# The last input tile's weights: one early load, or fifteen loads of a few partitions behind the fourth store

## The chip, the core and the metric

The kernel runs on one core of a Trainium2 chip. The core has compute engines with instruction queues of their own (the vector engine, DVE; the scalar engine, ACT; the tensor engine, PE; GpSimd, POOL), the SyncE queue (SP), and 16 DMA engines that move data between the chip's main memory (HBM) and the on-chip memory of 128 partitions. DMA transfers are issued by instructions on SyncE's and ScalarE's queues. The metric is the time of one execution on the device in microseconds (us); less is better. Before the change the median of three runs is 240.65 us (240.62 to 240.68).

## What is computed

Every token's row of 512 float32 numbers is written out twice, each copy multiplied by one of the token's two weights. The expert indices are an input but are not used.

```python
batch, seq, hidden, n_experts = 16, 1024, 512, 8     # k = 2
x_expanded = x[:, :, np.newaxis, :].repeat(k, axis=2)
weights = expert_weights[..., np.newaxis]
return (x_expanded * weights).astype(np.float32)
```

That is 33.55 MB of x in, 0.13 MB of weights in, and 67.11 MB out. There is one multiplication for each number written.

## The kernel before

The 16,384 tokens are spread over 128 partitions, 128 tokens to a partition. The work is cut into six input tiles: five of 24 tokens for each partition and a last one of 8 (`groups`, line 32). An input tile (`x_tile`, two buffers) is filled by DMAs that ScalarE's queue issues (line 82): the first tile in six pieces of 4 tokens, every other tile in one transfer. `load(i + 2)` at line 119 asks for the tile after next, once tile `i` has been worked through.

For each token and each of its two weights, one instruction multiplies a 128x512 block by one column of `w_tile` and writes it into an output buffer (`o_tile`, two buffers, 12 tokens each). Column `c` of `w_tile` is the counter: where `c % 3 == 2` ScalarE does it (line 100), otherwise VectorE (line 106), so that VectorE has 16 and ScalarE 8 of the 24 blocks in an output buffer. When a buffer is full, SyncE issues one store of it (line 115): two stores for each tile of 24 tokens and one for the last tile, eleven in all, ten of 6,144 KB and one of 4,096 KB. Buffers are used in turn, so the buffer of store 4 is written again for store 6, that of store 5 for store 7.

The weights come in three loads at the start, all issued by SyncE ahead of the stores: those of the first tile (line 53, 48 columns), those of the next four tiles (line 54, 192 columns), and those of the last tile (line 58, 16 columns: 64 bytes for each of 128 partitions).

Instructions of one queue run in the order in which they stand. The order and all semaphore waits are made by the framework that builds the kernel from this text: an instruction waits for the data it reads and for the buffer it overwrites. In the trace's records every DMA issue names the semaphore on which it counts, and the waits of an instruction name the semaphores waited for. There are eight of them for DMA transfers, and one each for ScalarE's and VectorE's instructions.

The change is around lines 58 (removed), 115 (the store, whose instruction is kept in a name) and 119 (after it).

Of the kernel before, what the change touches and what calls it, by code (L numbers as in the profile page):

```python
# [1 line left out]

# [4 lines left out]


@with_exitstack
def kernel(  # L10
    ctx: ExitStack,
    tc: tile.TileContext,
    x: bass.AP,
    expert_indices: bass.AP,
    expert_weights: bass.AP,
    out: bass.AP,
):
    nc = tc.nc

    batch, seq, hidden = x.shape  # L20
    k = expert_weights.shape[-1]
    P = nc.NUM_PARTITIONS
    ntok = batch * seq
    assert ntok % P == 0
    A_TOTAL = ntok // P

    f32 = mybir.dt.float32
    row = k * hidden
    TX = 24
    TO = 12  # L30

    groups = [[24], [24], [24], [24], [24], [8]]
    assert sum(sum(g) for g in groups) == A_TOTAL

    xf = x.rearrange("b s h -> (b s) h")
    of = out.rearrange("b s k h -> (b s) (k h)")
    wf = expert_weights.rearrange("b s k -> (b s) k")

    w_pool = ctx.enter_context(tc.tile_pool(name="w_pool", bufs=1))
    x_pool = ctx.enter_context(tc.tile_pool(name="x_pool", bufs=2))  # L40
    o_pool = ctx.enter_context(tc.tile_pool(name="o_pool", bufs=2))

    w_tile = w_pool.tile([P, A_TOTAL * k], f32)

    def rows(of_all, done, T):
        return of_all[done * P : (done + T) * P, :].rearrange(
            "(p a) n -> p (a n)", a=T
        )

    T0 = sum(groups[0])  # L50
    G = len([g for g in groups[1:] if sum(g) == T0])
    head = (1 + G) * T0
    nc.sync.dma_start(out=w_tile[:, : T0 * k], in_=rows(wf, 0, T0))
    nc.sync.dma_start(
        out=w_tile[:, T0 * k : head * k].rearrange("p (g n) -> p g n", g=G),
        in_=wf[T0 * P : head * P, :].rearrange("(g p a) n -> p g (a n)", g=G, p=P),
    )
    nc.sync.dma_start(
        out=w_tile[:, head * k :], in_=rows(wf, head, A_TOTAL - head)
    )  # L60

    tiles = []
    done = 0
    for group in groups:
        T = sum(group)
        a0 = 0
        for n in group:
            tiles.append((done, T, a0, n))
            a0 += n
        done += T  # L70

    loaded = []

    def load(i):
        if i >= len(tiles):
            return
        done, T, a0, n = tiles[i]
        x_tile = x_pool.tile([P, TX * hidden], f32)
        src = rows(xf, done, T)
        step = TX // 6 if i == 0 else n  # L80
        for at in range(0, n, step):
            nc.scalar.dma_start(
                out=x_tile[:, at * hidden : (at + step) * hidden],
                in_=src[:, (a0 + at) * hidden : (a0 + at + step) * hidden],
            )
        loaded.append(x_tile)

    for i in range(2):
        load(i)
    for i, (done, T, a0, n) in enumerate(tiles):  # L90
        x_tile = loaded[i]
        outr = rows(of, done, T)
        for t in range(n):
            if t % TO == 0:
                o_tile = o_pool.tile([P, TO * row], f32)
            for kk in range(k):
                c = (done + a0 + t) * k + kk
                o = t % TO * row + kk * hidden
                if c % 3 == 2:
                    nc.scalar.mul(  # L100
                        out=o_tile[:, o : o + hidden],
                        in_=x_tile[:, t * hidden : (t + 1) * hidden],
                        mul=w_tile[:, c : c + 1],
                    )
                    continue
                nc.vector.tensor_scalar(  # L106
                    out=o_tile[:, o : o + hidden],
                    in0=x_tile[:, t * hidden : (t + 1) * hidden],
                    scalar1=w_tile[:, c : c + 1],
                    scalar2=None,  # L110
                    op0=mybir.AluOpType.mult,
                )
            if (t + 1) % TO == 0 or t + 1 == n:
                at = t // TO * TO
                nc.sync.dma_start(  # L115
                    out=outr[:, (a0 + at) * row : (a0 + t + 1) * row],
                    in_=o_tile[:, : (t + 1 - at) * row],
                )
        load(i + 2)

# [1 line left out]
_INS = ['x', 'expert_indices', 'expert_weights']  # L122
_OUTS = [((16, 1024, 2, 512), 'float32')]


# [23 lines left out]
```

## Time and profile before

| what | value |
|---|---|
| median of three runs | 240.65 us |
| span of the profiled execution (its own time; the profile lists no other) | 238.9 us |
| data moved | 100.81 MB, 422 GB/s over the span |
| DVE busy | 69.0 us, 171 instructions of 0.48 us |
| ACT busy | 54.9 us, 85 multiplications of 0.71 us and one table load |
| stores | 11, from issue to landing 33.6 us in the median of the ten large |
| x loads | 11, of which 6 pieces of the first tile |
| weights loads | 96, 24 and 8 KB; 11.1, 2.9 and 13.2 us from issue to landing |
| issue of the stores on SyncE | 13.38 us for the first, 218.4 us for the last |

The span begins with the first instruction of the program and ends with the last. A line of the chain of waits gives start, duration and what the time was spent on. A line of the timeline gives start, stretch, engine (a q marks the engine's queue, where DMA issues and semaphore instructions stand), line, operation and tiles, how many of them, and in square brackets the idle time ahead of the first one with what ended it. A line of the table of stretches gives the stretch, its length, the busy time of DVE, ACT and POOL with the number of instructions, the clock of the tensor engine (not used here), the mean busy share of the DMA engines, and GB/s. The DMA share of a short stretch can come out a little over 1. In the page, the DMA row gives the busy share in tenths in 40 slices of 5.97 us, where 9 is 90% or more.

### The profile page before, as it was taken

Reading aid. Unit: us, or ns where it says so; the run is one execution under the profiler, and the core shown is the slowest. Engines: PE = TensorE matmul, PEld = TensorE weight load, DVE = VectorE, ACT = ScalarE, POOL = GpSimd, SP = SyncE. Lnnn points to the kernel's source line nnn. Section 1 sums busy time; section 2 is a strip of 40 time slices with the busy share of each in tenths; the row PEclk is TensorE's granted clock in tenths of the full one; section 3 lists DMA queues with packets and bytes.
Section 4 is the critical chain, followed back from the end, with each engine's and each line's share of the span. In section 5 each row is a group of like instructions: output and inputs, shape, how many; then the busy total and the mean of one; then the engine's idle time right before and its main releaser. Section 6 shows DMA issues by size and latency. Waiting matters only on the chain.

```text
span 238.9 us, 364 instructions
## 1 busy us (share of the span) xinstructions
DVE 69.0 (29%) x171; ACT 54.9 (23%) x86; POOL 0.2 (0%) x4
## 2 busy tenths in 40 slices
DVE  0890300004609100190063037003706406415000
ACT  0870300004308000170071034003406106213000
POOL 0000000000000000000000000000000000000000
DMA  6999999999999999999999999999989899999994
GB/s 244 420 443 395 495 395 395 494 428 395 428 494 395 413 494 411 395 446 469 403 411 502 395 420 453 436 411 428 469 379 496 381 428 469 436 411 428 436 439 197
DMA packets 3986, 100.81 MB, mean 422 GB/s; under 512 B 1168, under 2 KB 1168, under 8 KB 1168
## 3 DMA queue, kind: packets, MB, share of 16 engines
q1 hardware_dynamic: 2400, 67.24, 65.2%
q10 hardware_dynamic: 1584, 33.56, 33.1%
q14 instruction: 2, 0.02, 0.0%
HBM read 33.69 MB, written 67.11 MB: 422 GB/s over the span
## 4 chain that ended last, share of the span: by engine, by line
DMA 66%; DVE 13%; another core or an unknown queue 11%; issue 0%; DVEq 0%; SPq 0%
DMA out_dram<-o_tile 54%; DVE o_tile L106 13%; DMA x_tile<-in_x_dram 11%; DVEq L144 0%; DVEq L106 0%; SPq L115 0%
## 5 line engine op out<-in xcount | busy, mean ns | idle before, releaser
L106 DVE TENSOR_SCALAR o_tile<-x_tile,w_tile 128x512 f32<-128x512 f32 x171 | 69.0, 480 | 149.3 <-DMA out_dram<-o_tile 105.3
L100 ACT ACTIVATE o_tile<-x_tile,w_tile 128x512 f32<-128x512 f32 x85 | 53.6, 709 | 155.5 <-DMA out_dram<-o_tile 116.8
L100 ACT ACT_TABLE_LOAD x1 | 1.3, 1283 | 6.7 <-DMA x_tile<-in_x_dram 6.7
L133 POOL MEMSET const-bfloat16-1.0<- 128x1 bf16 x1 | 0.1, 101 | 0.0
L133 POOL MEMSET const-uint8-127<- 128x1 uint8 x1 | 0.1, 101 | 0.0
L133 POOL MEMSET const-float32-0.0<- 128x1 f32 x1 | 0.1, 98 | 0.2 <-issue 0.2
L133 POOL MEMSET const-float32-1.0<- 128x1 f32 x1 | 0.1, 98 | 0.0
## 6 DMA issues: line engine op xcount, KB each, us to landing
out_dram<-o_tile SPq DMA_DIRECT2D x10, 6144.0 KB, 33.6
x_tile<-in_x_dram ACTq DMA_DIRECT2D x4, 6144.0 KB, 43.9
x_tile<-in_x_dram ACTq DMA_DIRECT2D x6, 1024.0 KB, 10.6
out_dram<-o_tile SPq DMA_DIRECT2D x1, 4096.0 KB, 19.5
x_tile<-in_x_dram ACTq DMA_DIRECT2D x1, 2048.0 KB, 24.0
w_tile<-in_expert_weights_dram SPq DMA_DIRECT2D x1, 96.0 KB, 11.1
w_tile<-in_expert_weights_dram SPq DMA_DIRECT2D x1, 24.0 KB, 2.9
w_tile<-in_expert_weights_dram SPq DMA_DIRECT2D x1, 8.0 KB, 13.2
```

What stands on the lines that cost most here:

```text
L100: nc.scalar.mul(out=o_tile[:, o : o + hidden], in_=x_tile[:, t * hidden : (t + 1) * hidden], mul=w_tile[:, c : c + 1],)
L106: nc.vector.tensor_scalar(out=o_tile[:, o : o + hidden], in0=x_tile[:, t * hidden : (t + 1) * hidden], scalar1=w_tile[:, c : c + 1], scala ...
L133: nc = _bacc.Bacc("TRN2", target_bir_lowering=False, num_devices=1)
```

## The change

The load at line 58 is taken out. In its place stands a function that loads the same 16 columns in fifteen transfers, of 2, 3, 4, ... 15 and then 9 partitions (together 128), all issued by SyncE. It is called once, after the work of the second tile (`i == 1`) and after `load(3)`, inside a block that puts its instructions behind the instruction of the store issued last on the same queue, which is the fourth store. Nothing else is changed.

```diff
-    nc.sync.dma_start(
-        out=w_tile[:, head * k :], in_=rows(wf, head, A_TOTAL - head)
-    )
+    def last_weights():
+        src = rows(wf, head, A_TOTAL - head)
+        at = 0
+        for n in list(range(2, 16)) + [9]:
+            nc.sync.dma_start(
+                out=w_tile[at : at + n, head * k :], in_=src[at : at + n, :]
+            )
+            at += n
+        assert at == P
...
-                nc.sync.dma_start(
+                stored = nc.sync.dma_start(
                     out=outr[:, (a0 + at) * row : (a0 + t + 1) * row],
                     in_=o_tile[:, : (t + 1 - at) * row],
                 )
         load(i + 2)
+        if i == 1:
+            with tc.issue_after(stored.ins):
+                last_weights()
```

## The prediction

> **What bounds the kernel now.** I read the page first, then the chain of waits, then the timeline of instructions, then what SyncE's queue waited for, then the stretches.
>
> ```profile
> span 238.9 us, 364 instructions
> DVE 69.0 (29%) x171; ACT 54.9 (23%) x86; POOL 0.2 (0%) x4
> DMA  6999999999999999999999999999989899999994
> HBM read 33.69 MB, written 67.11 MB: 422 GB/s over the span
> w_tile<-in_expert_weights_dram SPq DMA_DIRECT2D x1, 8.0 KB, 13.2
> ```
>
> No compute engine is busy for a third of the span, and the 16 DMA engines are full in all but the first and last slices. A packet row tells how full: each 49,152-byte packet takes 1.815 us in the trace, 27.1 GB/s for an engine, 433 GB/s for sixteen. 100.81 MB at that rate is 232.8 us; start and tail make up the rest. So time is lost only where the DMA engines run dry, and won only by moving less.
>
> The chain of waits, in order of time, shows what feeds them:
>
> ```profile
> 100.89 6.43 DVE o_tile L106 x16
> 107.32 0.02 SPq L115
> 107.34 0.03 issue
> 107.37 33.72 DMA out_dram<-o_tile
> ```
>
> That is store 5. SyncE issues it at 107.34 and it lands at 141.1. It is on time because it is queued early: store 4 is still moving. The timeline shows when store 4 lands, since the next work takes over its o_tile buffer:
>
> ```profile
> 78.38 49.78 SPq L115 DMA_DIRECT2D out_dram<-o_tile  x3
> 78.41 0.36 ACTq L82 DMA_DIRECT2D x_tile<-in_x_dram  x1
> 100.85 5.01 ACT L100 ACTIVATE o_tile<-x_tile,w_tile 128x512 f32<-128x512 f32 x8 [24.04 <-DMA out_dram<-o_tile]
> 121.25 5.01 ACT L100 ACTIVATE o_tile<-x_tile,w_tile 128x512 f32<-128x512 f32 x8 [15.39 <-DMA out_dram<-o_tile]
> 127.86 0.35 ACTq L82 DMA_DIRECT2D x_tile<-in_x_dram  x1
> ```
>
> Store 3 landed just before 100.85, store 4 at 121.22 by its last semaphore event; the fourth x load (issued 78.41) at 115.32, the third at 86.26. No x load is issued between 78.41 and 127.86. So from about 119.8 (store 4's last packets) to 127.86 the only work the DMA engines have is store 5. Nothing covers it if it is late.
>
> ```profile
> SPq L115 <- DVE o_tile L106: 212.4, 11, 33.1
> ```
> ```profile
> 107.00:119.00 12.00, 0.31 (x1) 0.00 (x0) 0.00 (x0) 1.00 1.06 459
> 119.00:124.00 5.00, 2.65 (x7) 2.75 (x5) 0.00 (x0) 1.00 1.02 442
> 140.00:180.00 40.00, 12.85 (x32) 10.02 (x16) 0.00 (x0) 1.00 1.00 434
> 180.00:220.00 40.00, 17.29 (x43) 13.19 (x21) 0.00 (x0) 1.00 1.01 437
> ```
>
> SyncE's stores now wait for compute alone. The stretches (last but one number: DMA share) show no slack after 107 in which a loss could be made good.
>
> **A wait that the diff does not print.** In the records of the DMA issues every transfer counts on one of eight semaphores, taken strictly in turn over SyncE's and ScalarE's transfers together: 25 transfers, three rounds and one. A transfer that takes a semaphore again first waits for the transfer that had it before, also when both are on SyncE: store 1 waits for the semaphore of the second weights load, whose columns its data doesn't need. In the kernel before, this costs nothing, as the holder is always long landed. Fifteen loads in a row on eight semaphores go once around and nearly twice. Counted on with the third weights load gone from the round: x piece 6 / x1 / store 1 / x2 / store 2 / store 3 / x3 / store 4 are the last holders of the eight, and small loads 1 to 8 follow them in this order (x1 to x3: the second to fourth input tile). Load 4 waits for x2 (86.26), load 6 for store 3 (100.76), load 7 for x3 (115.32), and load 8 for **store 4, 121.22**. Whatever the order, fifteen loads cannot pass eight semaphores without meeting store 4's. All of them stand on SyncE's queue ahead of stores 5 to 11; store 5 is ready at 107.34 and has to wait, and behind it the vector and scalar engines, which need its o_tile buffer.
>
> **The change part by part.** *Removed at the start*, by SyncE's own timeline:
>
> ```profile
> 1.63 0.50 SPq L58 DMA_DIRECT2D w_tile<-in_expert_weights_dram  x1
> 13.38 205.39 SPq L115 DMA_DIRECT2D out_dram<-o_tile  x11
> ```
>
> One issue of 0.50 us on SyncE, which is then idle until 13.38, and on each DMA engine eight 64-byte packets of 11 ns and one semaphore packet of 9 ns, 0.10 us. SyncE's part is worth nothing (cover: the wait for store 1's data; without it, 0.5). The DMA engines' part is worth 0 to 0.10; I take 0.10, as they are full there.
>
> *Added traffic:* the same 128 packets, and between 128 and 240 semaphore packets instead of 16. If a load of n rows uses n engines, an engine that takes a row of every load has 15 x (11 + 9 ns) = 0.30 us. It falls into the hole below: nothing; without the hole, 0.2 more than was removed, so 0 to 0.2.
>
> *Added issues on SyncE.* Loads 1 to 7 go out between 78.8 and 115.7 while SyncE would be waiting anyway: nothing. Loads 8 to 15 go out after 121.22. The stores' issues take 0.332 us and the next instruction starts 0.045 later; the three weights loads start 0.43 and 0.47 apart, with ScalarE issuing beside them. Bounds for one: 0.25 (fewer rows than any issue shown) and 0.95 (the longest issue of an x piece, 0.898, and its gap). I take 0.40, near the SyncE rows: 8 x 0.40 = 3.2 us. Store 5 also needs load 8's semaphore: the smallest issue-to-landing in the trace is 2.9 us, inside the 3.2, and so a floor if issues are cheap.
>
> *Store 5.* 121.22 + 0.03 (release) + 3.2 + 0.1 (two waits already met, 28 to 50 ns each, and gaps) = issued at 124.55 instead of 107.34. From an issue to an idle ring's first packet the start shows 1.0 us (issue 0.73, first packet 1.73), so its packets start at 125.55. Store 4's packets end between 119.8 and 120.77, 120.2 on the mean (landing events, less the 0.45 between the last packet's end and the last event). Lost: 125.55 - 120.77 = 4.8 for the last engine and 5.35 for the mean; I take 5.1, as a common restart removes part of the engines' spread.
>
> *After it.* Tile 2's second half is computed from 121.25 as now, so the fifth x load and store 6 are issued at 127.9 as now; x4 alternates with more of store 5, store 5 lands some 9 us later (about 150), store 6 about 5 later. Store 7's data is ready near 157, when store 6 still has until about 169: nothing more runs dry, nothing is made good. The scalar and vector engines look at up to eight semaphores before the last tile: four pairs of 50 to 70 ns, at most 0.3 us at 214, hidden behind store 10, which moves until 228 (store 11 is issued at 218.4); without it, 0.3.
>
> *Sum:* span 238.9 + 5.1 - 0.1 = 243.9. The profile has no time of its own execution beside the span; the runs' median, 240.65, stands 1.75 above it, and I keep that: **245.6 us**.
>
> **Against the skill.** The row is the 2.9 us from issue to landing of the first weights load. The Trainium skill, "DMA: Bandwidth & Descriptors", section "Rules for kernel authors", says that many small transfers should be made one large one, as under 64 KB one pays mostly overhead; the same page fits about 2.0 us of fixed cost (for transfers issued by GpSimd). An estimate by that page, with fifteen of them in series, is 30 us more; by the row's reasoning only the eight late issues count, since the transfers overlap. The same page, section "Why a DMA increments its semaphore by 16 and not by 1", says that two transfers in flight on one semaphore can let a wait pass early, which is a reason for the waits that the records show.
>
> **The rivals.**
> 1. *SyncE is not held (not slower).* Point of decision: store 5's issue before about 118.7, 1.0 us ahead of store 4's last packets. If the loads waited only for x3 or for nothing, SyncE would be through at 115.32 + 8 x 0.40 = 118.5 at the latest and store 5 lose next to nothing: 240.65 - 0.1, or + 0.2, so 240.5 to 240.9. Against: store 1's wait, and 15 > 8. It also holds if the loads were placed early instead of behind store 4. Chance 0.09; a further 0.02 that the lighter start alone gains over 0.5 (the packets removed are worth 0.10).
> 2. *The late loads go one after the other.* Should each of the eight late loads wait for the landing of one just issued, 8 x 2.9 = 23 us stands in place of 3.2: 240.65 - 0.1 + 5.1 - 3.2 + 23.2 = 265.7. Against: loads 9 to 15 take the semaphores of loads 1 to 7, six of which were issued 20 us before. A partial form, one or two landings in the line, gives 248.5 to 251. Chance 0.06.
> 3. *The hold is shorter than priced.* Store 4 is among the eight holders in any order, so at least eight issues follow its landing; the hold shrinks only if these are cheap, load 8 lands in under 2.0 us and the common restart wins back much of the engines' spread: 2.5 to 3.2 lost, 243.1 to 243.8. Chance 0.03.
>
> **How the numbers follow.** The forecast case has 0.80. Its own range: cheapest issues, with load 8 landing in 2.0 (1.0 to the first packet and the 0.9 from there to the first weights load's first semaphore event) to 2.9, lose 3.5 to 4.5 (244.1 to 245.1); 0.55 an issue (the third weights load, 0.497, and its gap) loses 6.3 (246.8); 0.80, most of the way to the longest, 8.3 (248.8); 0.95 would be 250. The range 243.8 to 248.8 holds the forecast case but for a few parts in a hundred, and some of rivals 2 and 3. 0.2% is 0.48 us, about what a measurement of this kernel can tell from no change: faster 0.02, same 0.09, slower 0.89.
>
> **What would show it.** Right: SyncE's waits name DMA transfers at the loads' line; store 5 is issued near 124.5; the slice of the DMA row at 119 to 125 drops to few tenths, the other slices stay; packets go from 3986 to at least 4098; store 4's landing stays within 0.5 of 121.2. Wrong: store 5 still at 107, or the hole elsewhere, or a hole longer than 9 us.

## The result, and the profile after

The changed kernel takes 247.16 us (median of four runs, 247.07 to 247.76) against 240.67 us for the kernel before beside it. The ratio is 1.0279, 95% interval 1.0258 to 1.0300: 6.5 us slower. The forecast was 245.6 us, in a range of 243.8 to 248.8.

From the page of the changed kernel:

```profile
span 245.4 us, 378 instructions
DMA  6999899899998998999569999998999999999995
DMA packets 4098, 100.81 MB, mean 411 GB/s; under 512 B 1280, under 2 KB 1280, under 8 KB 1280
```

The DMA row, full before, has a gap in its 20th and 21st slice (a 5 and a 6, from 116.6 to 128.8 us). The bytes are the same; the packets are 112 more, all small ones.

What SyncE's queue waited for, in the changed kernel:

```profile
SPq L122 <- DVE o_tile L113: 173.7, 10, 33.1
SPq L62 <- DMA out_dram<-o_tile: 23.4, 2, 16.1
SPq L62 <- DMA x_tile<-in_x_dram: 16.6, 2, 12.2
```

Before, this queue waited for compute eleven times, 212.4 us in all. Now it does so ten times, 173.7 us, and 40.0 us of waiting stand at line 62, the small loads: two waits for stores and two for x loads. A load of 128 to 960 bytes needs neither. They are the waits for a semaphore's former holder: in the records of the DMA issues store 3 and load 6 name one semaphore, the fourth x load and load 7 a second, and store 4, load 8 and store 5 a third.

The timeline around store 4, of the changed kernel:

```profile
78.46 0.33 SPq L122 DMA_DIRECT2D out_dram<-o_tile  x1
78.84 45.62 SPq L62 DMA_DIRECT2D w_tile<-in_expert_weights_dram  x15
121.48 5.01 ACT L107 ACTIVATE o_tile<-x_tile,w_tile 128x512 f32<-128x512 f32 x8 [14.89 <-DMA out_dram<-o_tile]
124.58 3.86 SPq L122 DMA_DIRECT2D out_dram<-o_tile  x2
128.08 0.36 ACTq L89 DMA_DIRECT2D x_tile<-in_x_dram  x1
```

The fifteen loads occupy SyncE from 78.84 to 124.47. Store 5 is issued at 124.58, before it was 107.34. The chain of waits shows the last part of that in single steps (start, duration, what):

```profile
78.46 43.00 DMA out_dram<-o_tile
121.46 0.02 issue
121.47 0.27 SPq L62
121.74 0.04 issue
121.79 0.32 SPq L62
...
124.15 0.31 SPq L62
124.47 0.05 issue
124.52 0.03 SPq L122
124.55 0.03 issue
124.58 26.77 DMA out_dram<-o_tile
```

Store 4 lands at 121.46; then eight small loads go out one after the other, and only then store 5. The stretches of the changed kernel (DMA share, GB/s at the end) show what the DMA engines did:

```profile
107.00:119.00 12.00, 1.04 (x3) 0.00 (x0) 0.00 (x0) 1.00 1.04 451
119.00:124.00 5.00, 2.42 (x7) 2.52 (x5) 0.00 (x0) 1.00 0.07 21
140.00:180.00 40.00, 12.85 (x32) 10.02 (x16) 0.00 (x0) 1.00 1.00 434
180.00:220.00 40.00, 12.85 (x32) 10.02 (x16) 0.00 (x0) 1.00 0.99 427
```

Between 119 and 124 us they were busy for 7% of the time, where before it was all of it. Later stretches are as full as before and make nothing good.

The packet records give the sum. "Dry" below is the time that a DMA engine had no packet, summed over the sixteen and divided by 16; "slow packets" is what the packets of 8 KB and more took beyond the usual duration of their size (1.815 us for 49,152 bytes), summed and divided in the same way. Dry time in mid-run: none before, 4.92 us after, all of it between 119.4 and 125.6. At the tail it is 0.27 less than before. Slow packets: in the first 118 us 1.17 before and 1.34 after, most of it at the start; from 118 to 146 us 0.08 before and 1.52 after. 4.92 - 0.27 + 0.17 + 1.44 is 6.3 of the 6.5; of these, the dry time is explained by the late store, and the slow packets are not explained yet.

### The profile page after: what moved, and what is told of

The parts are those of the page before. It is cut to its first block, busy times and chain, and to the rows that moved or that the text cites. A ratio compares the mean times of both kernels' runs of the same rounds, so it can differ in the third digit from the quotient of the medians.

```text
span 245.4 us, 378 instructions
## 1 busy us (share of the span) xinstructions
DVE 69.0 (28%) x171; ACT 54.9 (22%) x86; POOL 0.2 (0%) x4
## 4 chain that ended last, share of the span: by engine, by line
DMA 78%; DVE 10%; SPq 1%; ACTq 1%; issue 0%; DVEq 0%
DMA out_dram<-o_tile 69%; DVE o_tile L113 10%; DMA x_tile<-in_x_dram 9%; SPq L62 1%; ACTq L89 1%; DVEq L154 0%; DVEq L113 0%; SPq L122 0%
```

## The experiments

Four accounts of the loss are compared. The theory (A): fifteen transfers in a row on eight semaphores have to wait for the transfers that hold them, store 4 among these; SyncE stands, store 5 is late, and the DMA engines run dry. The rivals: (B) the small transfers cost by themselves, 0.43 us each; (C) the place costs; (D) the time for which SyncE is held costs, whatever is in flight meanwhile. A second question came with the result: where the 1.5 us of slow packets come from. Experiments on that start with the staggered x load. A time is set against the kernel before in the same comparison.

| run | us | ratio, 95% interval | store 5 issued | dry in mid-run | slow packets at the fifth x load |
|---|---|---|---|---|---|
| before | 240.65 | | 107.34 | 0 | 0.08 |
| changed kernel | 247.16 | 1.0258 to 1.0300 | 124.58 | 4.92 | 1.43 |
| one load moved | 240.52 | 0.9983 to 1.0002 | 108.15 | 0 | 0.07 |
| six loads | 241.15 | 1.0011 to 1.0030 | 115.84 | 0 | 0 |
| seven loads | 244.03 | 1.0123 to 1.0153 | 121.81 | 2.23 | 1.63 |
| fifteen from GpSimd | 241.64 | 1.0025 to 1.0055 | 108.11 | 0.02 | 0.21 |
| six behind store 5 | 240.44 | 0.9975 to 0.9993 | 107.74 | 0 | 0 |
| fifteen behind store 5 | 245.88 | 1.0199 to 1.0230 | as before | 5.03, near 150 to 155 | 0.05; 1.0 at the sixth x load |
| fifteen at the start | 245.46 | 1.0134 to 1.0224 | | 1.4, near 5 to 7 | 0.13 |

### One load, moved

```diff
-        for n in list(range(2, 16)) + [9]:
+        for n in [128]:
```

> The load of the last tile's 16 columns stays whole (128 partitions, one transfer) and is issued behind store 4. Theory A (the loads pass all eight semaphores, so SyncE waits for store 4 and the DMA engines run dry): one load takes one semaphore whose holder landed long ago, store 5 is issued at 107.3 as before, 240.5 to 240.9. Rival B (each extra small transfer costs about 6.5 / 15 = 0.43 us wherever it stands): 240.7, one load as before. Rival C (the place behind store 4 is what costs): 245 to 247.

240.52 us against 240.60: no difference. The place alone costs nothing (C falls), and neither does it gain.

### Six loads, and seven

```diff
-        for n in list(range(2, 16)) + [9]:
+        for n in [22, 22, 21, 21, 21, 21]:                 # six
+        for n in [19, 19, 18, 18, 18, 18, 18]:             # seven
```

> Six loads (22, 22, 21, 21, 21, 21 partitions) behind store 4. Theory A: load 6 waits for store 3 and store 5 itself for the fourth x load (115 us); store 5 is issued at 115.4 instead of 107.3, still ahead of store 4's last packets at 119; no dry stretch, 240.5 to 240.9. Rival B: 240.65 + 5 x 0.43 = 242.8. Rival D (the time for which SyncE is held past 107.3 is the price, 6.5 for 17.2 us): 8.1 us held, 243.7.

> Seven loads (19, 19, 18, 18, 18, 18, 18 partitions) behind store 4, one more than six. Theory A: load 7 takes the fourth x load's semaphore and store 5 that of store 4, so store 5 is issued at 121.5 and its packets start near 122.5: some 2.1 us dry. If the slow packets that followed the dry stretch in the changed kernel (1.5 us per engine) belong to any restart, 244.0; if they belong to the long stretch or the fifteen loads, 242.5. Rival B: 0.43 more than six loads. Rival D: 14.2 us held, 246.0.

Six loads: 241.15 us, 0.25 above the upper end of what A gave, and 1.6 below B, 2.5 below D. SyncE's waits and its timeline in this kernel:

```profile
SPq L122 <- DMA x_tile<-in_x_dram: 16.0, 1, 16.0
77.07 22.70 SPq L62 DMA_DIRECT2D w_tile<-in_expert_weights_dram  x6
115.84 103.38 SPq L122 DMA_DIRECT2D out_dram<-o_tile  x7
```

SyncE stood 16.0 us in front of store 5, for an x load, the fourth, whose data the store has nothing to do with; in the records the two name one semaphore. Store 5 went out 8.5 us later than before, at 115.84. That was still ahead of store 4's last packets, so no DMA engine stood idle. The remaining 0.5 us is left open: the trace has no dry time, and 0.4 us per engine more of slow packets than before, but over half of that lies in the first 30 us, ahead of the six loads.

One load more, and the records show store 5 on the semaphore of store 4. The stretch and the chain of waits of the kernel with seven loads:

```profile
119.00:124.00 5.00, 2.14 (x6) 2.24 (x4) 0.00 (x0) 1.00 0.42 169
```
```profile
78.38 43.35 DMA out_dram<-o_tile
121.73 0.02 issue
121.75 0.03 SPq L122
121.78 0.03 issue
121.81 23.19 DMA out_dram<-o_tile
```

Store 5 goes out at 121.81 and 2.23 us per engine are dry. The time, 244.03 us, is the 244.0 that A gave when the slow packets come with any restart: 2.23 + 1.63 less 0.8 at an evener tail are 3.1 of the 3.4 lost. One small load more costs 2.9 us here; the six before it together cost 0.5. So B falls: the price is not one per transfer wherever it stands, it lies in which semaphore is met. (From seven to fifteen loads it is 3.1 us more, 0.39 a load: there eight issues stand between store 4's landing and store 5, and nothing covers them.)

### The same fifteen loads from GpSimd

```diff
-            nc.sync.dma_start(
+            nc.gpsimd.dma_start(
...
-            with tc.issue_after(stored.ins):
+            mark = nc.gpsimd.tensor_copy(
+                out=spare[:, :], in_=o_tile[:, TO * row - 1 : TO * row]
+            )
+            with tc.issue_after(mark.ins):
```

> The same fifteen loads, but issued by GpSimd, behind a copy of one number per partition out of store 4's buffer, so at about 78.5 us; they count on semaphores of GpSimd's own. Theory A: the transfers are all there, SyncE's queue is free, store 5 is issued at 107.3: 240.5 to 241.0. Rival B: 246 to 247. Rival D: 240.7.

241.64 us, 0.6 above what A gave and 4.4 below B. Lines of its timeline:

```profile
78.04 4.20 POOL L63 DMA_DIRECT2D w_tile<-in_expert_weights_dram  x8
90.08 0.52 POOL L63 DMA_DIRECT2D w_tile<-in_expert_weights_dram  x1 [7.84 <-DMA w_tile<-in_expert_weights_dram]
97.38 0.52 POOL L63 DMA_DIRECT2D w_tile<-in_expert_weights_dram  x1 [6.78 <-DMA w_tile<-in_expert_weights_dram]
```

GpSimd's fifteen loads show the same turn: eight go out at once, then each waits until its semaphore's former load has landed. But nothing of consequence stands behind them on that queue. Store 5 went out at 108.11. Some 1.0 us above the kernel before remains: the page has 337 packets more (small packets take 0.3 us more per engine), and the trace has slow packets of 0.3 us near 100 us; the rest is open.

### Held, but covered

```diff
-        for n in list(range(2, 16)) + [9]:
+        for n in [22, 22, 21, 21, 21, 21]:
...
+                if i == 2 and t + 1 == TO:
+                    with tc.issue_after(stored.ins):
+                        last_weights()
         load(i + 2)
-        if i == 1:
-            with tc.issue_after(stored.ins):
-                last_weights()
```

> Six loads (22, 22, 21, 21, 21, 21 partitions) behind store 5 instead of store 4. Load 6 waits for store 4 (121.2 us), store 6 for store 5 (141 us), so SyncE is held until 141 and store 6 is issued 13 us late; but the fifth x load, which ScalarE issues at 127.9, still has some 9 us of packets then. Theory A (only a dry stretch of the DMA engines costs): store 6 near 141.3, no dry stretch, 240.6 to 241.3. Rival D (the time for which SyncE is held is the price, 6.5 for 17.2 us): 245.5.

240.44 us against 240.69, 0.16 under the range that A gave. The interval, 0.07 to 0.25% below, does not hold nought, but the size is what the prediction called no difference (0.2%). Its timeline:

```profile
108.13 13.24 SPq L62 DMA_DIRECT2D w_tile<-in_expert_weights_dram  x6
127.72 0.34 ACTq L89 DMA_DIRECT2D x_tile<-in_x_dram  x1
141.06 0.37 SPq L122 DMA_DIRECT2D out_dram<-o_tile  x1
```

Store 6 was ready at 127.7, like the x load in the second line, and went out at 141.06: held for 13.3 us, three quarters of store 5's 17.2 in the changed kernel. It cost nothing, since the x load still had packets until store 6's came. D falls: the hold by itself had no price here.

### Fifteen behind store 5

The edit is the one above with the list of fifteen left as it is.

> The fifteen loads behind store 5 instead of store 4. Theory A: in the turn of the semaphores load 8 now follows the fifth x load (issued by ScalarE at 127.9), so SyncE is held until that has landed, near 150.5 when it has the DMA engines to itself from 141 on; eight issues later, near 154, store 6 goes out and its packets start near 154.9. Dry from 150 to 155: 4.3 to 4.8 us. If slow packets follow when the last x load (16 KB rows) starts beside store 7 or 8 (theory L, engines in step): 1.0 to 1.6 more, 245.9 to 247. If they belong to the fifth x load beside store 5 (rival P): none, 244.9 to 245.6. Rival B (0.43 a load): 247 with no dry stretch.

245.88 us. The chain of waits of this kernel:

```profile
128.19 22.59 DMA x_tile<-in_x_dram
150.77 0.02 issue
150.79 0.27 SPq L62
...
153.48 0.31 SPq L62
...
153.90 0.37 SPq L122
```

Load 8 waited for the fifth x load, landing at 150.77, and store 6 followed at 153.90, against 150.5 and 154 expected from counting the turn; 5.03 us were dry. The trace has 1.4 us more of slow packets than before in all and 1.0 less at an evener tail: 5.4 of the 5.5 us by which this profiled execution is longer. This is A at another place and with another holder.

### Fifteen at the start

```diff
-        if i == 1:
-            with tc.issue_after(stored.ins):
-                last_weights()
...
+    last_weights()
```

> The fifteen loads stand where the one load stood, at the start, and not behind store 4. Theory A (the loads take turns on the semaphores with the x pieces, so the second x piece has to wait for the first one to land at 5.2 to 5.8 us and the DMA engines have nothing but weights until its first packet 1.0 us after the issue): a dry stretch of some 1.8 us near 5 to 7, 242.0 to 243.0. Rival B (each extra small transfer costs 0.43 wherever it stands): 246 to 247. If neither: 240.7.

245.46 us, 2.5 above the upper end of what A gave and only 0.5 below B, so this time taken alone would speak for B; the trace does not. The hole is there, but with its slow packets it is only half of the loss. The stretches:

```profile
2.00:6.00 4.00, 0.27 (x1) 0.00 (x0) 0.00 (x0) 1.00 0.80 279
6.00:12.00 6.00, 3.62 (x10) 0.00 (x0) 0.00 (x0) 1.00 0.88 331
235.00:240.00 5.00, 0.00 (x0) 0.00 (x0) 0.00 (x0) 1.00 0.67 288
240.00:243.00 3.00, 0.00 (x0) 0.00 (x0) 0.00 (x0) 1.00 0.05 22
```

The second x piece waited for the first, and its packets began at 6.7 us: 1.4 us dry per engine, and 0.9 of slow packets more than before in the first 30 us. The rest is at the other end. The sixteen engines' last events of the last store came between 238.69 and 242.95 us (before: 236.21 to 237.98): the last engine came 3.9 us after the median of the sixteen, the next one 2.1, and the store waited for them. Why the engines end so unevenly was not settled, and whether the early hole is the cause was not tested.

### The fifth x load, staggered and in step

The slow packets of the changed kernel are the packets in flight as the fifth x load joins: all sixteen of store 5 that began between 130.97 and 131.12 took 2.18 to 2.96 us instead of 1.815, and twelve of the x load's first sixteen up to 3.31. In the kernel before, the corresponding sixteen store packets began within 1.51 us (fifteen of them within 0.67) and none was slow. Theory L: the restart puts the engines in step, and that makes the packets slow. Rival P: the fifth x load beside store 5 is slow after any restart.

```diff
+        if i == 2:
+            with tc.issue_after(scaled.ins):               # scaled: the last nc.scalar.mul
+                for j, n in enumerate([14, 11, 8, 5, 2]):  # control: [16, 16, 16, 16, 16]
+                    nc.scalar.dma_start(
+                        out=spare[:n, j * 256 : j * 256 + 256],
+                        in_=rows(xf, 0, 24)[:n, j * 256 : j * 256 + 256],
+                    )
         load(i + 2)
```

> The changed kernel, and ahead of the fifth x load ScalarE issues five loads of 1 KB rows, of 14, 11, 8, 5 and 2 partitions, into a spare tile that nobody reads, so that the 16 DMA engines come to the fifth x load at different times. The question is the slow packets near 131 to 137 us (1.5 us per engine beyond 1.815 each) that follow the restart. Theory L (they come from all engines turning to the x load in the same moment, as the dry stretch has put them in step): they fall below 0.6 us and the time to 245.9 to 246.4. Rival P (the fifth x load's first packets beside store 5's are slow whatever the engines do, after any restart): 1.3 to 1.7 us of slow packets stay, 247.1 to 247.5.

> The control: the same five loads of 1 KB rows with 16 partitions each, so every DMA engine comes to the fifth x load equally late, still in step, near 138 to 140 us and beside store 6's first packets rather than store 5's. Theory L: 1.3 to 1.7 us of slow packets stay, moved to near 140, 247.0 to 247.5. Rival P: the x load no longer begins beside store 5; slow packets below 0.6, 245.9 to 246.4. If they stay near 131: it is the first read of any kind after the restart.

247.89 and 248.02 us, slow packets 1.45 and 1.69 us. Neither says anything on L or P: ScalarE's queue issued the five loads between 122.2 and 125.1, into the dry stretch, so the x load was not moved at all (its first packets at 133.3 and 133.6).

A second pair ties them to the last vector instruction ahead of store 6.

```diff
+            nc.vector.tensor_scalar(
+                out=seen[:, :], in0=spare[:, :],
+                scalar1=o_tile[:, TO * row - hidden - 1 : TO * row - hidden],
+                scalar2=None, op0=mybir.AluOpType.mult,
+            )
+            for j, n in enumerate([14, 11, 8, 5, 2]):      # control: [16, 16, 16, 16, 16]
+                ahead = nc.scalar.dma_start(
+                    out=spare[:n, j * 64 : j * 64 + 64],
+                    in_=rows(xf, 0, 24)[:n, j * 64 : j * 64 + 64],
+                )
+        with tc.issue_after(ahead.ins) if i == 2 else ExitStack():
+            load(i + 2)
```

> The stagger again, now tied to the vector engine's last block ahead of store 6 (a product of 320 spare numbers per partition that nobody uses), so the five loads of 14, 11, 8, 5 and 2 partitions (256 B rows) are issued from 128.3 on, directly ahead of the fifth x load, which follows near 130.2. Each of them takes a turn between store 5's packets of 1.8 us, so the DMA engines come to the x load up to some 9 us apart. Theory L: the x load's own slow packets vanish and slow packets fall below 0.7 us in all, 246.0 to 246.7. Rival P: 1.3 to 1.7 us stay, 247.0 to 247.7.

> The control to it: the same five loads with 16 partitions each, so all DMA engines come to the fifth x load together, later by the same five turns. Theory L: 1.3 to 1.8 us of slow packets stay, at the x load's start or at that of the first of the five, 247.1 to 247.9. Rival P: below 0.7, 246.0 to 246.7.

Control: 248.02 us, 0.1 above the range that L gave. The x load joined at 149.9 beside store 6, and the slow packets went with it: 0.04 us from 130 to 146, 1.63 from 146 to 160. P falls, and it falls a second time in the run with fifteen loads behind store 5: there the fifth x load joined before the hole with 0.05 us, and the sixth, after the hole and beside store 7, came with 1.0 (the sixteen store packets in flight began between 180.29 and 180.45).

Stagger: 250.26 us, above both ranges, and 2.5 us of slow packets. (Another 2.3 us of dry time than before are at its end, where the engines' last events lie between 243.39 and 248.18 us.) L as it was put falls here. Groups of DMA engines came to the x load between 138 and 151 us, and each group was slow at its own turn, down to two engines at 150.7 that took 3.4 us for a packet. The stretches, ahead the kernel before, then the changed kernel, the control and the stagger, show it as GB/s that a full DMA share moves:

```profile
126.00:140.00 14.00, 1.77 (x5) 0.26 (x1) 0.00 (x0) 1.00 0.95 407
```
```profile
126.00:140.00 14.00, 2.00 (x6) 0.49 (x1) 0.00 (x0) 1.00 1.00 386
```
```profile
140.00:156.00 16.00, 6.43 (x16) 5.02 (x8) 0.00 (x0) 1.00 1.04 403
```
```profile
140.00:156.00 16.00, 6.42 (x16) 5.01 (x8) 0.00 (x0) 1.00 1.02 387
```

407 / 0.95 is 428 GB/s; the others are 386, 388 and 379.

### Phases spread

A stagger by whole turns leaves the beat: in that run the packets of a group still began within 0.1 to 0.3 us of each other. The last run spreads the engines within one packet.

```diff
+        if i == 2:
+            with tc.issue_after(scaled.ins):
+                at = 0
+                for n in [16, 16, 16, 12, 8, 4]:
+                    nc.scalar.dma_start(
+                        out=spare[at : at + n, :],
+                        in_=rows(xf, 0, 24)[at : at + n, :3584],
+                    )
+                    at += n
         load(i + 2)
```

> The changed kernel, and behind its share of tile 2's second half ScalarE issues six loads of 14 KB rows of x into a spare tile that nobody reads, of 16, 16, 16, 12, 8 and 4 partitions. They fall into the dry stretch; the last three run into store 5's start on 12, 8 and 4 partitions, so that four groups of DMA engines should come out of it some 0.5 us apart, within one packet of 1.8 us. That is what the stagger by whole turns did not do: there the engines' packets still began within 0.1 us of each other. Theory L' (slow packets come when all engines stand at the same point of a packet, in phase, as another stream joins): slow packets near the fifth x load's start fall from 1.5 to below 0.7 us per engine; the loads themselves add up to 0.8, so 246.2 to 247.2. If the phase is not the cause: 1.3 to 1.9 us stay, 247.4 to 248.4.

The engines came out of the hole 1.2 us apart (store 5's first packets at 127.08 to 128.29), and the slow packets around the x load (130 to 146 us) fell to 0.43 us, as L' (the engines in phase within one packet) had it. The time, 252.63 us (four runs, 251.08 to 255.94; interval of the ratio 1.0467 to 1.0619), is 5 us above the range of L': the spare loads' 72 packets of 14 KB took 1.06 us on the mean where 14,336 bytes at 27.1 GB/s are 0.53, 4.8 us per engine in all, only part of it in the hole (24 of the 72 began after 130 us), and store 5's own first packets beside them had 0.47 us of slow packets. So the common beat as the cause is supported by one number in a run with a disturbance of its own, and is not shown.

## Why the prediction was right, point by point

- *The eight semaphores and the order of holders.* Right, load for load: load 4 waited for the third x load, load 6 for store 3, load 7 for the fourth x load, load 8 for store 4, as the waits at line 62 and the issue times (84.6, 101.5, 114.0, 121.5 us) show. The counting also gave the turning point between six and seven loads, and load 8's holder behind store 5.
- *Eight issues at 0.40 us, 3.2 in all.* They took 0.27 to 0.38 each with 0.04 between, 3.05 us; the issues grow with the number of partitions from 9 to 15. Load 8 landed at 122.75, 1.3 us after its issue: the floor of 2.9 that I took from the first weights load was too high, but did not decide.
- *Store 5 issued at 124.55, first packet at 125.55.* Measured 124.58 and 125.44. Store 4's landing, 121.22 before, was at 121.46.
- *Lost 5.1 us.* 4.92 dry; the common restart did even out the tail, by 0.27.
- *"Nothing more runs dry, nothing is made good."* Right, but this is the step with the missing term. It took the packets after the restart at their old duration; they took 1.44 us per engine longer as the fifth x load joined, which the seven-load kernel repeats with 1.63. The sum, 245.65 before rounding, came out 1.5 too low. It lacks 1.44 for these packets, 0.17 for other slow packets and 0.2 that the records leave open, and took off 0.1 for a removal that did not show; its hole was 0.45 too dear (5.1 for 4.92 - 0.27).
- *The range.* 247.16 lies within 243.8 to 248.8, but not for the reason that the range gives. Its part above 245.6 was made for dearer issues (0.55 us each for 246.8), and the issues were cheaper than 0.40. That the missing term fitted into this room was luck; its cause is open.
- *Removed at the start, 0.1.* Too small to see: the one load moved measured 0.08 below, with an interval that holds nought.
- *Rivals.* The first (SyncE not held) is what six loads and GpSimd's queue make of it, 241.15 and 241.64: close to its 240.5 to 240.9, and somewhat over. Its turning point, store 5 out before about 118.7, stood between the 115.84 of six loads and the 121.81 of seven. The second (a landing for each late load) did not happen: loads 9 to 15 found their holders landed. Of the third, cheaper issues and an early load 8 were there by 0.2 us, the tail's gain by 0.3.
- *The skill's rule.* The Trainium skill, "DMA: Bandwidth & Descriptors", section "Rules for kernel authors", counsels against many small transfers for their overhead. Here six of them cost 0.5 us and fifteen on an idle queue 1.0; what made fifteen dear is that SyncE stood until store 4 had landed and then had eight of them to issue, 3.05 us, ahead of store 5 and with nothing else in flight. In its section "Why a DMA increments its semaphore by 16 and not by 1" the page says that a transfer issued by SyncE posts one increment for each DMA engine that it uses, and that this number divides the partitions; the 112 packets more agree: 128 increments for 2 + 3 + ... + 15 + 9 partitions in place of 16.

## What to carry to other kernels

Count transfers against the semaphores they take in turn: a run of as many transfers as there are semaphores is a wait for everything in flight on the queues that share them (here SyncE's and ScalarE's; GpSimd's loads waited for each other only), whatever the transfers move, and what stands behind it on its queue can be late. Such a hold costs nothing while another queue still has packets for the DMA engines, and costs the dry stretch when it has none, with 0.9 to 2.5 us of slow packets on top in these runs, so the first question is what is still in flight when the hold ends. Small or early work of this kind belongs on a queue that nothing urgent stands behind, or in one transfer.

## What the runs showed of the hardware that was not expected

After a dry stretch of 2 to 5 us the DMA engines restart together, within 0.14 to 0.18 us (in the kernel before they stood up to 1.5 us apart at the fifth x load), and when the other queue's transfer then joins, the packets in flight take up to twice as long (3.6 us): 1.4 to 1.7 us per engine in five kernels with a hole ahead of an x load of 48 KB rows, whether 5 or 22 us after the restart, 2.5 in a sixth, and 1.0 with 16 KB rows, against 0 to 0.2 in the runs without a hole. It moved with the joining transfer, not with the place. Whether the common beat is its cause is open: groups of two engines were as slow as all sixteen; the one run that broke the beat had 0.43. And in the profiled execution with a hole at the very start, one engine ended 3.9 us behind the median after 230 us of full load; the staggered run, without such a hole, ended as unevenly, so the cause is open.
